# Two-layer adaLN trunk on one core: modulation vectors collected in the rows of one tile and transposed once per sublayer, attention's products regrouped, gate columns in a tile of their own

## The chip, the cores and the metric

The kernel runs on one core of a Trainium2 chip. The metric is the device time of one execution in microseconds (us), the median of several. TensorE (PE) multiplies, VectorE (DVE) and ScalarE (ACT) do elementwise work, SyncE (SP) issues the loads.

## The reference, cut to what matters

One sequence of 256 tokens, width 1024, float32, two layers. Each layer is FFN, token mixing, FFN; each sublayer normalizes, applies a shift and a scale, and adds its result under a gate. Shift, scale and gate come from a vector c (adaLN): nine vectors of 1024 a layer, each a product of silu(c) with a 1024 x 1024 matrix.

```python
mod = (jax.nn.silu(c) @ ada_w[l] + ada_b[l]).reshape(B, 3, 3, 1, D)
n = _modulate(_rmsnorm(h, norm_g[l, 0]), mod[:, 0, 0], mod[:, 0, 1])
h = h + 0.5 * mod[:, 0, 2] * _swiglu(n, ffn_w_in[l, 0], ffn_w_out[l, 0])
n = _modulate(_rmsnorm(h, norm_g[l, 1]), mod[:, 1, 0], mod[:, 1, 1])
z = n @ mix_w_in[l]
zq, zkv, zg, zuv, zga, zgb = jnp.split(z, IN_SPLITS, axis=-1)
...
nsa_gates = jax.nn.sigmoid(zg).reshape(B, S, NSA_HEADS, 3)
y_a = _nsa(q, kv[:, :, 0], ..., nsa_gates, ...)      # 8 heads, 3 branches
y_b = _gmlp(zuv, ...)                                # u * (W_s v + b)
merged = jax.nn.sigmoid(zga) * (y_a @ proj_a[l]) + jax.nn.sigmoid(zgb) * (y_b @ proj_b[l])
h = h + mod[:, 1, 2] * (merged @ w_out[l])
n = _modulate(_rmsnorm(h, norm_g[l, 2]), mod[:, 2, 0], mod[:, 2, 1])
h = h + 0.5 * mod[:, 2, 2] * _swiglu(n, ffn_w_in[l, 1], ffn_w_out[l, 1])
```

The FFN is 2816 wide (SwiGLU). zg has 24 columns, zuv 1024 (u and v).

## The kernel before, in words

**Products.** An fp32 product is made of three matmuls on split operands: weight and activation are each cut into `hi` (rounded) and `lo` (the rest), and hi·hi, hi·lo and lo·hi are summed in PSUM. Most matmuls move 256 columns (the tokens) against a 128x128 weight block.

**Stream.** The class Stream loads the weights, 128x1024 pieces of 512 KB, through 18 slots W and 8 slots X (some 1088 wide, since the v weights were 1072 columns). SP issues the loads in the order of the list of items. `_split` makes hi on ACT (L134) and lo on DVE (L135), a few weights ahead of their use. Among the weights stand *ada items*: 512 KB of an adaLN matrix, which DVE multiplies with a column of silu(c) and adds to an accumulator (L252 the first, L255 the seven others of a set). The table `ada_plan` says in which sublayer (0 to 5: FFN, mix, FFN, FFN, mix, FFN) the items of which set are streamed, and `interleave` spreads them between two positions of the list.

**Sets.** A complete set waits in `ready`. `ada_step` is called between an FFN's groups of matmuls: it has four matmuls sum the accumulator over the partitions (L282; the profile counts eight), ACT copies the sum to a tile `adas` (L286), and the next call has PE transpose that tile twice (L267) and DVE add the bias, giving the tile `md` (L271). There are 16 such sets.

**FFN.** `in_mm` (L617) makes two products of 24 matmuls into a bank R, `out_mm` (L563) adds 24 matmuls into the banks A, in turn. **Entering a sublayer** (`enter`): h is updated from the banks A, products with uhi/ulo (L456, 258 columns) start on a not yet normalized h while the statistics are made, and `top` and `bottom` (L487, L488, L491) then make nhi and nlo from h and the row `rsb` (ACT, L475).

**Mix.** `tok_mm` (L796) makes q, k, v for 128 tokens at a time; v's weights held 536 columns, as two products of 268, the last 24 of them the gate. `blk_mm` (L809) and `proj_mm` (L1011) make the other projections and fill PE between the steps of attention. Attention runs over pairs `pr` of heads: `st_scores` (L1116), softmax on DVE and ACT (L1125, L1127), `st_scale` (L1135 to L1139), `st_trans` (L1144), `st_pv` (L1154, L1156). The constants of a layer (w1, wsT, ln, bs) lie in slots X and were loaded together near the end of the FFN ahead of the mix; wsT is masked by L966.

**What sets the order.** PE, SP and GpSimd run in the order of the program text. On DVE and ACT a scheduler orders the work by readiness and priority.

```python
        for pr in range(9):
            if pr >= 1:
                for i in (2 * pr - 2, 2 * pr - 1):
                    st_trans(i)
            if pr < 8:
                st_scores(pr)
...
            next(fill)
...
            if pr >= 1:
                for i in (2 * pr - 2, 2 * pr - 1):
                    st_pv(i)
```

## Time and profile before

| what | value |
|---|---|
| median of 3 runs | 1154.71 us (1152.73 to 1157.96) |
| profiled execution | 1160.77 us, its span 1159.0 us |
| mean granted TensorE clock | 0.987 |
| first FFN / entering / mix 0 | 64 to 216 / 216 to 229 / 229 to about 400 us |
| second and third FFN | 417 to 594 and 607 to 782 us |
| mix 1 / last FFN | 782 to about 964 / 976 to 1147 us |
| read from HBM | 275.49 MB, 239 GB/s over the span |

The span is what the profiler recorded between the first and the last instruction; 1.8 us of that execution lie around it. Views of the profile name instructions by engine and line (L617), with the output and inputs of the program (`R<-nhi,hi`), and `x48` is a count. The ends of matmuls are modelled, so the pace of matmuls is read from their starts: the pieces of the chain that ended last follow each other without a gap, and a piece's time divided by its count is the step from one matmul to the next. A wait's row names who waited for whose result.

### The profile page before, as it was taken

To read this page: it belongs to the slowest core of one execution; us is meant where nothing else is said; L and a number is where in the kernel's file an instruction comes from. 1 tells how busy PE (TensorE), PEld (TensorE's weight loads), DVE (VectorE), ACT (ScalarE), POOL (GpSimd) and SP (SyncE) were. 2 spreads that over 40 slices of the span, in tenths; PEclk is the share of its full clock that TensorE was granted. 3 is DMA by queue.
4 is the path that set the end of the run, shared out by engine and by line. 5 is a ranking of instruction groups with operands and counts; after the bars stand their busy time and mean duration, and the time that the engine had idled before them with its cause. 6 is when DMAs were issued, how large, how long until landed. Compare 5 with 4: busy or idle time off the path is not lost. (4 is left out here: it accounts for less than half of the span.)

```text
span 1159.0 us, 23635 instructions
## 1 busy us (share of the span) xinstructions
PE 1137.9 (98%) x9630; PEld 1096.2 (95%) x9630; DVE 879.7 (76%) x1514; ACT 599.4 (52%) x1020; POOL 9.6 (1%) x13
## 2 busy tenths in 40 slices
PE   8999999989899999999999999999999999999998
PEld 6999999979799999999999999998899899999998
DVE  4998786778977799777579977767886778856543
ACT  3474444655575575444465444356656647544432
POOL 0000000000000000000000000000000000000000
PEclk8999999999999999999999999999999999999998
DMA  9979598438744659987647977974443366766600
GB/s 364 406 255 379 213 356 318 171 114 312 271 161 144 242 195 374 334 296 282 243 159 278 372 264 275 360 284 149 183 147 127 119 224 223 259 215 242 223 26 37
DMA packets 77180, 278.07 MB, mean 240 GB/s; under 512 B 8592, under 2 KB 9104, under 8 KB 77072
## 3 DMA queue, kind: packets, MB, share of 16 engines
q1 hardware_dynamic: 77072, 276.57, 65.1%
q8 instruction: 75, 1.23, 0.4%
q14 instruction: 33, 0.27, 0.1%
HBM read 275.49 MB, written 1.05 MB: 239 GB/s over the span
## 5 line engine op out<-in xcount | busy, mean ns | idle before, releaser
L135 DVE TENSOR_TENSOR lo<-raw,hi 128x1024 fp32r<-128x1024 f32 (+1 forms) x366 | 443.0, 1217 | 127.2 <-ACT hi L134 107.0
L134 ACT ACTIVATE hi<-raw 128x1024 fp32r<-128x1024 f32 (+1 forms) x366 | 381.0, 1052 | 273.3 <-PE R L617 67.0
L563 PE MATMUL A<-s1r,hi 128*128 128x256 f32 x1408 | 255.2, 279 | 0.0
L617 PE MATMUL R<-nhi,hi 128*128 128x256 f32 x1152 | 229.6, 281 | 0.0
L617 PE MATMUL R<-nhi,lo 128*128 128x256 f32 x1152 | 227.1, 279 | 0.0
L617 PE MATMUL R<-nlo,hi 128*128 128x256 f32 x1152 | 226.8, 279 | 0.0
L563 PEld LDWEIGHTS A<-s1r,hi 128*128 128x128 f32 x1408 | 218.9, 189 | 0.2 <-DVE s1r L555 0.2
L563 PE MATMUL A<-s1r,lo 128*128 128x256 f32 x704 | 196.0, 278 | 0.0
L617 PEld LDWEIGHTS R<-nhi,hi 128*128 128x128 f32 x1152 | 174.8, 188 | 5.8 <-issue 5.8
L617 PEld LDWEIGHTS R<-nlo,hi 128*128 128x128 f32 x1152 | 175.3, 189 | 0.0
L617 PEld LDWEIGHTS R<-nhi,lo 128*128 128x128 f32 x1152 | 175.0, 189 | 0.0
L255 DVE SCALAR_TENSOR_TENSOR acc<-raw,sc,acc 128x1024 f32<-128x1024 f32 x112 | 143.4, 1281 | 24.5 <-DMA raw<-in_ada 23.7
L563 PEld LDWEIGHTS A<-s1r,lo 128*128 128x128 f32 x704 | 132.3, 188 | 0.0
L583 ACT ACTIVATE s<-R 128x256 f32<-128x256 f32 x75 | 28.3, 377 | 105.1 <-PE R L617 105.1
L809 PE MATMUL A<-nhi,hi 128*128 128x256 f32 x256 | 74.8, 292 | 0.0
L809 PE MATMUL A<-nhi,lo 128*128 128x256 f32 x256 | 71.8, 280 | 0.0
L809 PE MATMUL A<-nlo,hi 128*128 128x256 f32 x256 | 71.8, 280 | 0.0
L554 ACT ACTIVATE s1r<-s 128x256 fp32r<-128x256 f32 x88 | 36.2, 412 | 47.9 <-DVE s L585 46.7
L585 DVE TENSOR_TENSOR s<-s,R 128x256 f32<-128x256 f32 x75 | 31.2, 416 | 37.1 <-ACT s L583 37.0
L809 PEld LDWEIGHTS A<-nhi,hi 128*128 128x128 f32 x256 | 49.0, 191 | 3.9 <-issue 2.3
L809 PEld LDWEIGHTS A<-nhi,lo 128*128 128x128 f32 x256 | 48.7, 190 | 0.0
L809 PEld LDWEIGHTS A<-nlo,hi 128*128 128x128 f32 x256 | 48.6, 190 | 0.0
(258 smaller groups left out, 1627.5 us busy)
## 6 DMA issues: line engine op xcount, KB each, us to landing
raw<-in_win SPq DMA_DIRECT2D x170, 512.0 KB, 5.7
raw<-in_ada SPq DMA_DIRECT2D x144, 512.0 KB, 5.7
raw<-in_mixw SPq DMA_DIRECT2D x92, 512.0 KB, 3.6
raw<-in_wou SPq DMA_DIRECT2D x88, 512.0 KB, 5.4
raw<-in_mixv SPq DMA_DIRECT2D x8, 536.0 KB, 5.7
w<-in_w SPq DMA_DIRECT2D x8, 512.0 KB, 8.5
raw<-in_win SPq DMA_DIRECT2D x8, 384.0 KB, 9.8
h<-in_xT SPq DMA_DIRECT2D x2, 512.0 KB, 5.5
```

The source lines that it names most:

```text
L134: self.nc.scalar.activation(hi[:, :n], raw[:, :n], AF.Copy)
L135: self.nc.vector.tensor_sub(lo[:, :n], raw[:, :n], hi[:, :n].bitcast(F32))
L255: V.scalar_tensor_tensor(a, raw[:, :D], sc[:, kb:kb + 1], a, op0=ALU.mult, op1=ALU.add)
L554: A.activation(hi_out, src, AF.Copy)
L563: T.matmul(accs[db // 2][:, (db % 2) * S:(db % 2 + 1) * S], w[:, db * 128:(db + 1) * 128], xx, start=(first and i == 0 and p == 0 and db % ...
L583: A.activation(s_, r[:, 0:S], AF.Silu)
L585: V.tensor_mul(g_, s_, r[:, S:2 * S])
L617: T.matmul(r[:, ab * S:(ab + 1) * S], W[:, c0:c0 + 128], xx[:, k], start=(i == 0 and ab == 0), stop=(i == 23), skip_group_check=True)
L809: T.matmul(r[:, b * S:(b + 1) * S], w[:, k], xx[:, k], start=(b == 0 and k == 0 and p == 0), stop=(k == 7 and p == 2), skip_group_check=True)
```

## The change

1. **Sets.** The sum of a set is now made with `hot`, a tile of zeros with one column of ones: its shifted slice puts the k-th set of the sublayer in row k of each 32-row group. The first set is copied by ACT into the tile `rows["t"]`, later ones are added to it by DVE. `ada_flush` transposes that tile once per sublayer, ahead of the FFN's last product (in a mix, within its output product), and makes all `md` tiles.
2. **Plan.** The first FFN streams five sets (it had four), mix 0 one (it had two), spread over more of its weights.
3. **Layer constants.** Only mp is loaded in the FFN; w1 goes into the mix's list at position 5, wsT, ln and bs at position 9.
4. **Gate.** v's weights are 512 columns, one product; the gate's 24 columns (padded to 32) are a weight tile of 128x256 with hi and lo in one slot. Its result is computed as 64 x 256 and brought to tokens by two small matmuls, `gzs` between them.
5. **Attention.** `st_pv` of pair pr − 2, `st_trans` of pr − 1 and `st_scores` of pr now follow each other, then both fills. `st_scale` treats both heads of a pair in one reciprocal and one product.
6. **Slots.** All slots are 1024 wide. The four X0, X1, X2, X5 take raw weights alone. `top` reads the row in PSUM and no longer waits for ACT's copy.

```diff
+EVEN_SLOTS = ("X0", "X1", "X2", "X5")
...
-            sh, hi = self._take(f"hi{i}", F32R, n)
-            sl, lo = self._take(f"lo{i}", F32R, n)
-            self.nc.scalar.activation(hi[:, :n], raw[:, :n], AF.Copy)
-            self.nc.vector.tensor_sub(lo[:, :n], raw[:, :n], hi[:, :n].bitcast(F32))
+            sh, hi = self._take(f"hi{i}", F32R)
+            sl, lo = self._take(f"lo{i}", F32R) if n > 256 else (None, hi)
...
+            self.nc.scalar.activation(hv, rv, AF.Copy)
+            self.nc.vector.tensor_sub(lv, rv, hv.bitcast(F32))
...
+    hot = cp.tile([128, 64], F32, name="hot")
+    V.memset(hot, 0.0)
+    V.memset(hot[:, 31:32], 1.0)
...
     def ada_step(now=False):
 
         clock[0] += 1
-        while summed:
-            si, m, sm = summed.pop(0)
+        while ready and (now or clock[0] >= ready[0][2]):
+            si, m, _ = ready.pop(0)
+            k = len(summed)
             p = rbank()
-            for f in range(2):
-                T.transpose(p[:, f * 128:(f + 1) * 128], sm[:, f * 128:(f + 1) * 128], ident)
+            for t in range(4):
+                T.matmul(p[32 * t:32 * t + 32, 0:256], hot[:, 31 - k:63 - k], acc[si, m][:, t * 256:(t + 1) * 256],
+                         start=True, stop=True, tile_position=(0, 32 * t))
             with tc.high_priority(PRIO_M):
+                if k == 0:
+                    rows["t"] = tp.tile([128, 256], F32, tag="adas", name=f"adas{si}_{m}")
+                    A.activation(rows["t"], p[:, 0:256], AF.Copy)
+                else:
+                    V.tensor_add(rows["t"], rows["t"], p[:, 0:256])
+            summed.append((si, m))
+
+    def ada_flush():
+
+        p = rbank()
+        for f in range(2):
+            T.transpose(p[:, f * 128:(f + 1) * 128], rows["t"][:, f * 128:(f + 1) * 128], ident)
+        with tc.high_priority(PRIO_M):
+            for k, (si, m) in enumerate(summed):
...
-        while ready and (now or clock[0] >= ready[0][2]):
-            si, m, _ = ready.pop(0)
-            p = rbank()
-            for t in range(4):
-                T.matmul(p[32 * t:32 * t + 32, 0:256], ones[:, 0:32], acc[si, m][:, t * 256:(t + 1) * 256],
-                         start=True, stop=True, tile_position=(0, 32 * t))
-            sm = tp.tile([128, 256], F32, tag="adas", name=f"adas{si}_{m}")
-            with tc.high_priority(PRIO_M):
-                A.activation(sm, p[:, 0:256], AF.Copy)
-            summed.append((si, m, sm))
...
-    ada_plan = {0: [(0, 2), (1, 0), (1, 1), (1, 2)], 1: [(2, 0), (2, 1)], 2: [(2, 2), (3, 0), (3, 1), (3, 2)],
+    ada_plan = {0: [(0, 2), (1, 0), (1, 1), (2, 0), (2, 1)], 1: [(1, 2)], 2: [(2, 2), (3, 0), (3, 1), (3, 2)],
...
-        ws = interleave(ws, extra, *((20, 18) if kind == "mix" else ((12 if idx == 0 else 14), 6)))
+        if kind == "mix":
+            ws = interleave(ws, extra, MIX_A, len(ws) - MIX_B)
+            ws.insert(9, layer_loads(idx, 2))
+            ws.insert(5, layer_loads(idx, 1))
+        else:
+            ws = interleave(ws, extra, 10 if idx == 0 else 14, 6)
         if kind == "ffn" and idx % 2 == 0:
-            ws.insert(len(ws) - 8, layer_loads(idx // 2))
+            ws.insert(len(ws) - 8, layer_loads(idx // 2, 0))
...
-            V.scalar_tensor_tensor(tt_[db], h[:, db], A_[:, db:db + 1], rsb, op0=ALU.mult, op1=ALU.mult)
+            V.scalar_tensor_tensor(tt_[db], h[:, db], A_[:, db:db + 1], aux[:, 256:512], op0=ALU.mult, op1=ALU.mult)
...
-                ada_step()
+                ada_step(k >= NF - TAIL)
+        if summed:
+            ada_flush()
         out_mm(*range(NF - GROUP, NF))
...
-            tok_mm(vb, 536, c, st.next(), [(0, 268), (268, 268)])
+            tok_mm(vb, 512, c, st.next(), [(0, 512)])
+
+        gz = bank("A1")
+        W = st.next()
+        wg = W[0][:, 0:512].rearrange("p (k c) -> p k c", c=64)
+        for k in range(8):
+            for p in range(2):
+                T.matmul(gz[0:64, 0:S], wg[:, k], x[p][:, k], start=(k == 0 and p == 0), stop=(k == 7 and p == 1),
+                         skip_group_check=True)
...
+        gzs = tp.tile([64, 256], F32, tag="s1", bufs=8, name=f"gzs{l}")
+        A.activation(gzs, gz[0:64, 0:S], AF.Copy)
...
+        for tt in range(2):
+            T.matmul(gz[:, 256 + tt * 24:280 + tt * 24], gzs[:, tt * 128:(tt + 1) * 128], cst_t[0:64, C_SEL:C_SEL + 24],
+                     start=(tt == 0), stop=True, skip_group_check=True)
...
-        for pr in range(9):
-            if pr >= 1:
+        for pr in range(10):
+            if pr >= 2:
+                for i in (2 * pr - 4, 2 * pr - 3):
+                    st_pv(i)
...
+            if 1 <= pr < 9:
                 for i in (2 * pr - 2, 2 * pr - 1):
                     st_trans(i)
             if pr < 8:
                 st_scores(pr)
-                for i in (2 * pr, 2 * pr + 1):
-                    st_scale(i)
+                st_scale(pr)
...
-        acc_mm(accs, Ws, False, True, lambda db: ada_step(db == 2) if db in (0, 2, 4) else None)
+        acc_mm(accs, Ws, False, True, lambda db: ada_step(True) if db == 0 else ada_flush() if db == 3 and summed else None)
```

What this does to the order shows at three places. The first is PE in the attention loop of mix 0, an iteration in its middle (L809 is a block fill and L837 the same line after the change; L1154 and L1156 are pv, after the change L1199 and L1201). Before, a fill stands on both sides of pv:

```order
L809 MATMUL A_300_4047<-nlo_2956,hi_3723 128x256
L1154 MATMUL A_261_3759<-s_289_3998,VK_3244 64x256
L1156 MATMUL A_261_3759<-s_289_3998,VK_3244 64x128
L1154 MATMUL A_261_3759<-s_291_4004,VK_3244 64x256
L1156 MATMUL A_261_3759<-s_291_4004,VK_3244 64x128
L809 MATMUL A_301_4085<-nhi_2955,hi_3798 128x256
```

PE after the change, at the same place (L1189 is the transposes, L1157 the scores):

```order
L837 MATMUL A_292_4034<-nlo_2974,hi_3770 128x256
L1199 MATMUL A_258_3738<-s_282_3957,VK_3292 64x256
L1201 MATMUL A_258_3738<-s_282_3957,VK_3292 64x128
L1199 MATMUL A_258_3738<-s_284_3963,VK_3292 64x256
L1201 MATMUL A_258_3738<-s_284_3963,VK_3292 64x128
L1189 MATMUL R_293_4066<-cst_t,s_288_3976 128x128 x3
L1189 MATMUL R_295_4072<-cst_t,s_289_3981 128x128 x3
L1157 MATMUL R_297_4078<-VK_3292,qT_3279 128x128
```

Pv moved from between two fills to ahead of the transposes and scores; the two fills then follow each other. The second place is DVE in the first iteration of that loop, from the scaling of the first probabilities on. Before (L252 and L255 are ada items, L135 lo splits, L1138 and L1139 the scaling):

```order
L252 TENSOR_SCALAR acc_1_3716<-raw_3598,sc 128x1024
L1138 TENSOR_SCALAR s_266_3774<-s_266_3774,rc_3785 128x128
L1135 RECIPROCAL rc_3790<-nmax_3779 128x2
L1139 TENSOR_SCALAR s_266_3774<-s_266_3774,rc_3785 128x256
L1136 TENSOR_TENSOR rc_3790<-rc_3790,gts_3424 128x2
L555 TENSOR_TENSOR ybl_3712<-s_257_3707,ybh_3711 128x512
L1138 TENSOR_SCALAR s_268_3780<-s_268_3780,rc_3790 128x128
L1139 TENSOR_SCALAR s_268_3780<-s_268_3780,rc_3790 128x256
L255 SCALAR_TENSOR_TENSOR acc_1_3716<-raw_3604,sc,acc_1_3716 128x1024
L135 TENSOR_TENSOR lo_3724<-raw_3673,hi_3723 128x1024
```

and after (L265 is an ada item, L142 a lo split, L1183 and L1184 the scaling):

```order
L265 SCALAR_TENSOR_TENSOR acc_2_3215<-raw_3593,sc,acc_2_3215 128x1024
L1178 RECIPROCAL rc_3763<-nmax_3752 128x4
L1180 TENSOR_TENSOR rc_3763<-rc_3763,gts_3416 128x4
L142 TENSOR_TENSOR lo_3810<-raw_3665,hi_3809 128x1024
L1183 TENSOR_SCALAR s_263_3753<-s_263_3753,rc_3763 128x128
L1184 TENSOR_SCALAR s_263_3753<-s_263_3753,rc_3763 128x256
L1183 TENSOR_SCALAR s_264_3758<-s_264_3758,rc_3763 128x128
L1184 TENSOR_SCALAR s_264_3758<-s_264_3758,rc_3763 128x256
L142 TENSOR_TENSOR lo_3886<-raw_3706,hi_3885 128x1024
```

The items there are one per iteration instead of two to three, and the half of gMLP's split (L555) left that place. The third place is DVE where mix 0 is entered. Before, one lo split (L135) stands there, ahead of the statistics (L400) and the modulated rows (L487, L491):

```order
L135 TENSOR_TENSOR lo_3012<-raw_2671,hi_3011 128x1024
L400 TENSOR_SCALAR var_2896<-A_182_2893 128x2
L414 TENSOR_SCALAR s_185_2924<-cst_t,rstd_2898 128x128 x2
L487 SCALAR_TENSOR_TENSOR s_187_2957<-h,md_1_2357,rsb_2929 128x256 x2
L487 SCALAR_TENSOR_TENSOR s_188_2962<-h,md_1_2357,rsb_2929 128x256 x2
```

After (L142 splits, L1007 the mask on wsT, L513 the modulated rows):

```order
L142 TENSOR_TENSOR lo_3024<-raw_2659,hi_3023 128x1024
L426 TENSOR_SCALAR var_2914<-A_180_2911 128x2
L142 TENSOR_TENSOR lo_3037<-raw_2673,hi_3036 128x1024
L440 TENSOR_SCALAR s_183_2942<-cst_t,rstd_2916 128x128 x2
L142 TENSOR_TENSOR lo_3069<-raw_2797,hi_3068 128x1024
L1007 TENSOR_TENSOR wsT_3029<-wsT_3029,cst_t 128x1024
L513 SCALAR_TENSOR_TENSOR s_185_2975<-h,md_1_2737,A_180_2911 128x256 x2
```

Three splits and the mask now stand there, and the modulated rows read PSUM (A) instead of rsb.

## What I predict

> **What bounds the kernel now.** The profile's page is read first: busy times, and the groups and transfers that carry prices below.
>
> ```profile
> PE 1137.9 (98%) x9630; PEld 1096.2 (95%) x9630; DVE 879.7 (76%) x1514; ACT 599.4 (52%) x1020; POOL 9.6 (1%) x13
> L135 DVE TENSOR_TENSOR lo<-raw,hi 128x1024 fp32r<-128x1024 f32 (+1 forms) x366 | 443.0, 1217 | 127.2 <-ACT hi L134 107.0
> L563 PE MATMUL A<-s1r,hi 128*128 128x256 f32 x1408 | 255.2, 279 | 0.0
> L617 PE MATMUL R<-nhi,hi 128*128 128x256 f32 x1152 | 229.6, 281 | 0.0
> L563 PE MATMUL A<-s1r,lo 128*128 128x256 f32 x704 | 196.0, 278 | 0.0
> L255 DVE SCALAR_TENSOR_TENSOR acc<-raw,sc,acc 128x1024 f32<-128x1024 f32 x112 | 143.4, 1281 | 24.5 <-DMA raw<-in_ada 23.7
> L585 DVE TENSOR_TENSOR s<-s,R 128x256 f32<-128x256 f32 x75 | 31.2, 416 | 37.1 <-ACT s L583 37.0
> raw<-in_mixw SPq DMA_DIRECT2D x92, 512.0 KB, 3.6
> ```
>
> TensorE (PE) is busy 98% of the span, so time can only come from how fast it steps, and from its few waits. The list of PE's waits comes second (us in total, times, longest):
>
> ```profile
> PE R L1144 <- DVE s L1138: 4.7, 2, 4.4
> PE A L796 <- DVE lo L135: 3.5, 3, 2.3
> ...
> PE R L456 <- DVE lo L135: 1.0, 1, 1.0
> ...
> PE R L456 <- ACT hi L134: 0.8, 1, 0.8
> PE A L617 <- ACT nhi L488: 0.6, 1, 0.6
> ```
>
> Then the chain that ended last, in order of time (start, us, what), around the last ada set:
>
> ```profile
> 1101.76 5.44 PE R L617 x48
> ...
> 1109.92 0.57 PE R L282 x8
> 1110.49 5.65 PE R L617 x48
> 1116.14 2.73 PE A L563 x24
> 1118.87 0.22 PE R L267 x2
> 1119.09 16.96 PE R L617 x144
> ```
>
> The same 256-column matmul has two paces. Before the transposes of L267 it steps every 5.44/48 = 113.3 ns; the set's sums (L282) leave that as it is. After the two transposes it steps every 16.96/144 = 117.8 ns, 4% slower, until something else interrupts. The table by windows, PE alone, over every stretch of the four FFNs with the slow pace (19 windows; the first, the longest, the last), and one fast stretch:
>
> ```profile
> 126.40:143.10 16.70, 16.70 (x145) 1.00 0.57 209
> ...
> 607.20:652.00 44.80, 44.80 (x383) 1.00 0.84 320
> ...
> 1119.10:1147.30 28.20, 28.20 (x242) 1.00 0.00 1
> sum 318.40, PE 318.40; mean PE 16.76
> 976.70:1109.80 133.10, 133.10 (x1176) 1.00 0.63 224
> ```
>
> Granted clock is 1.00 in both, so this is no throttling. Of these stretches 12 begin behind a pair of transposes, 6 behind a set's sums that were entered slow, and one (607.2) with the sublayer.
>
> The table by windows (span, PE busy, PEld, DVE, ACT, POOL, clock, DMA share, GB/s) for the two attention loops, three stretches at half clock, and two FFNs:
>
> ```profile
> 293.20:380.50 87.30, 82.64 (x687) 75.50 (x687) 73.31 (x200) 54.95 (x131) 0.00 (x0) 0.96 0.53 182
> 862.40:941.60 79.20, 79.20 (x685) 73.06 (x685) 56.81 (x177) 49.59 (x124) 0.00 (x0) 1.00 0.37 128
> 242.10:245.60 3.50, 3.50 (x23) 2.38 (x25) 2.34 (x3) 2.13 (x3) 0.00 (x0) 0.51 0.12 47
> 313.80:320.60 6.80, 5.65 (x28) 4.92 (x29) 6.76 (x18) 2.56 (x4) 0.00 (x0) 0.50 0.94 313
> 788.30:791.70 3.40, 3.40 (x18) 3.40 (x18) 3.40 (x9) 1.75 (x3) 0.00 (x0) 0.50 0.01 2
> 64.00:215.00 151.00, 150.99 (x1309) 148.61 (x1309) 121.60 (x145) 72.01 (x107) 0.00 (x0) 1.00 0.81 299
> 607.00:782.00 175.00, 175.00 (x1512) 172.28 (x1513) 142.08 (x175) 80.63 (x117) 0.00 (x0) 1.00 0.82 305
> ```
>
> A wait of 2.3 us (L796) or more is followed by some 3.4 us at clock 0.5, so each such wait costs about 1.7 us more than the list says.
>
> **The change, part by part.** The sum is made on the profiled execution, 1160.8 us, 6.1 us above the median of 1154.7; the same gain is then taken from the median.
>
> (A) Pace. Transposes stay only in a flush, ahead of the last 48 matmuls of a sublayer; the sums leave a fast stretch fast. All slow stretches at the fast pace: 318.4 × (1 − 113.3/117.8) = 12.2 us. Four flushes leave 48 matmuls slow each, 4 × 48 × 4.5 ns = 0.9. The stretch from 607.2 to the first transposes at 661 (some 53 us, 2.0 us of gain) began slow without transposes, behind the nhi wait of 0.6, and I leave it. **−9.3**; ends 0 and −12.2.
>
> (B) Sixteen pairs of transposes become five: 11 × 0.22 = **−2.4**. In exchange eleven sets are added to the row tile on DVE, which the nearest row (L585, 128x256 with a PSUM input) puts at 0.42 us each; they lie beside PE, which needs the tile only at the flush. Without that cover a flush would wait 0.4.
>
> (C) Attention of mix 0. Equal matmuls (x687, x685) take 87.3 us there and 79.2 in mix 1, which has no ada items. Sixteen items fall ahead of and into its first iterations; DVE fills 6.76 of 6.80 us there, and the transposes wait 4.4 us for the scaled probabilities. Eight items remain, one per iteration as the order shows. One iteration then asks DVE for about 1.28 + 2 × 1.22 beside its softmax; mix 1 pays 56.8/79.2 of the time without the item, and 7 × 1.28 = 9 us more is 83%. **−8.1**; ends 0 and −8.1.
>
> (D) Starts of the mixes. The first projections (L796) wait three times, 3.5 us in all, for a lo split that stands behind the normalization on DVE: twice at mix 0, the longer 2.3, and once at mix 1. The 2.3 is followed by 3.5 us at half clock (1.75): 5.25. The splits now stand ahead of it, three of them, as the order shows. What is late next: wsT, whose mask multiply (L1007, the old L966, formerly inside the FFN, a 128x1024 operation like L135's 1.2 us) now stands between the splits and the first modulated rows. Its load goes out when the FFN's last product frees a slot. The 96 entering matmuls, twice the 5.79 us quoted under rival 4, come before the rows, and a load lands in 3.6 us (in_mixw): several us to spare. If it came later than that, PE would wait as long. I take **−4.7**, a short wait left over (ends −5.25, +3). Entering mix 1, the fourth weight's hi and lo came amid the h updates: waits 0.8 and 1.0 and 1.7 of half clock; they now come ahead of them: **−3.5** (ends 0, −3.5).
> The Trainium skill, "TensorE: Matmul & The Clock Gate", Part 1, has the clock fall only behind an idle window of some 3.4 us. By it the half clock behind 2.3 us has another cause and may stay, and its −4.7 would be −2.95 (the sum −25.6); the trace shows half clock behind every wait of that size, and the sum goes by the trace.
>
> (E) Attention order. One iteration of mix 1 from the chain:
>
> ```profile
> 895.54 0.66 PE R L1144 x6
> ...
> 896.98 2.94 PE A L809 x24
> 899.92 0.59 PE A L1154 x4
> 900.50 0.22 PE A L1156 x4
> 900.72 3.02 PE A L809 x24
> ...
> 917.39 0.84 PE R L1144 x6
> ...
> 828.58 11.77 PE A L796 x93
> ```
>
> The 24 matmuls behind pv take 3.02 us: 24 × 117.8 = 2.83 and 0.19 of re-entry. At the fast pace they are 24 × 113.3 = 2.72. With pv, transposes and scores in a row, the second fill continues the first: −0.30 at best; if the 0.19 only moves to the joint between pv and transposes, −0.11. I take −0.2 × 16 iterations = −3.2. What it adds: transposes now wait for a softmax covered by two fills alone. With 24-matmul fills that is 5.7 us, enough; with the 12-matmul fills at the end of the loop, where the row of 0.84 against 0.66 already waits 0.18, the cover falls by pv's 0.8 us, so +0.2 to +0.5, twice per layer: +0.8 to +2. **−2.4**; ends −4.8 and +2.
> The Trainium skill, "TensorEngine Tiling (Array Packing)", Key Properties, says that a change of tiling mode, not of tile, drains TensorE. There are four changes of mode per iteration before and after (scores use 64 rows, pv 64 columns), so by it no joint is saved and (E) would be 16 × −0.11 + 0.8 = −1; the trace's re-entry of 0.19 behind pv agrees.
>
> (F) V and gate. The v product was 96 matmuls of 268 columns, 11.77/93 = 126.6 ns each, 12.1 us a layer. It becomes 48 of 512 columns. The nearest row of that width:
>
> ```profile
> 815.50:826.50 11.00, 11.00 (x48) 1.00 0.19 69
> ```
>
> so 48 take 11.0. The gate adds 16 at 113 ns (1.8), two small matmuls (0.3) and a wait for the copy between them (ends 0 and 1, taken 0.5; four key transposes lie in between, and behind the waiting pair stand PE's block fills, which need nothing of it). 11.0 + 2.6 − 12.1 = +1.5 a layer: **+3.0** (ends +2, +5).
>
> The sum: −9.3 − 2.4 − 8.1 − 4.7 − 3.5 − 2.4 + 3.0 = **−27.4**: 1133.4 for a profiled execution like this one, 1127.3 against the median, written as 1127.
>
> **The rivals.**
> 1. **The slow pace stays.** That transposes set it is a correlation: 12 of 15 followed, and 607.2 began slow with none. If a set's own sums or the sublayer's start set it, (A) is 0: 1137 us. If today's fast FFN stretches turn slow too (1408 + 704 + 3 × 1152 = 5568 matmuls in the groups quoted, three equal products of L617, less 318.4/0.1178 = 2700 slow ones: 2870 × 4.5 ns = 13): 1150.
> 2. **The first FFN becomes bound by its stream.** It takes 40 items for 32: DVE 121.6 + 8 × 1.28 = 132 of 151 us, 87%. Against it: the third FFN carries 40 at 81% with PE busy 175.00 of 175.00. For it: its window is shorter. Each stall would be like that at mix 1's start, 1.8 + 1.7 us; three are 10.5: 1138; with rival 1, 1147.
> 3. **The moves trade wait for wait:** wsT late, transposes late by 0.5 us in all 16 iterations (+8), the mixes' starts not cured ((D) 0, so +8.2), (C) half (+4): 1127.3 + 20.2 = 1147.5.
> 4. **Slower: a third pace.** All slots become 1024 wide, so weights and moving tiles lie at other addresses. This row of 258-column matmuls shows that such a pace exists:
>
> ```profile
> 964.19 5.79 PE R L456 x48
> ```
>
> 5.79/48 = 120.6 ns, 2.4% over the slow pace for 0.8% more columns. If the layout set it for the 5568 FFN matmuls, each would lose 5.1 ns against the mean of the two paces (115.5): +28, with (A) lost: 1127.3 + 9.3 + 28.4 = 1165. It decides the sign from some 3500 matmuls on (18.1/5.1 ns). Against it: sums and products of one layout already run at both paces, so the pace is not the layout's alone.
> 5. **It doesn't do what it says:** the scheduler's DVE order could undo the placement; the order shows the splits and items moved, so only their arrival is open: within 0.5%, 1152.
>
> **How the numbers follow.** Forecast 0.50 (its own range 1117 to 1135), rival 1 0.22, rival 2 0.08, rival 3 0.08, rival 4 0.06, rival 5 0.06. A measurement of this kernel can tell about 0.5% from no change, 5.8 us: faster is below 1149, slower above 1160.5. Faster: 0.50, most of rival 1 (0.18) and of 2 (0.07), a third of 3 (0.03) = 0.78. Slower: rival 4 and a rest of 3, 0.08. Same: 0.14. The best ends of all terms (−12.2 − 2.4 − 8.1 − 5.25 − 3.5 − 4.8 + 2 = −34.3) give 1120, a little more room below for paces I can't see: 1116. Above, the range takes in rivals 1 and 2 together: 1148.
>
> **What would show it.** (A): in the chain, FFN stretches of 5.44 us per 48 right up to the flush; 5.65 there would refute it. (B): L267's line with a third of its count. (C): mix 0's loop within 2 us of mix 1's, no wait of the transposes for the scaling over 1 us. (D): no L796 or L456 entry above 0.5 in the list of waits and no clock of 0.5 at the mixes' starts; an L1007 wait for wsT's DMA would be the failure. (E): an iteration of 7.9 to 8.1 us. (F): v and gate near 13.6 us a layer. The prediction is wrong if the paces follow something else than the transposes, since a third of the gain hangs on them.

## The result, and the profile after

The changed kernel takes 1126.44 us (median of 4 runs, 1125.87 to 1127.76) beside 1156.34 us for the kernel before (1152.73 to 1158.89): a ratio of 0.9745, 95% interval 0.9714 to 0.9776. A second set of runs gave 1126.84 us and 0.9738 (0.9706 to 0.977). The forecast was 1127 us. The time is right, and so are most of the sums; two of the reasons given for them are not, as the experiments show.

The whole list of PE's waits after the change (us in total, times, longest):

```profile
PE R L715 <- DVE s L713: 2.0, 1, 2.0
PE A L773 <- ACT nhi L762: 1.5, 1, 1.5
PE R L434 <- DVE ones L234: 1.1, 1, 1.1
PE R L733 <- DVE md L759: 0.9, 1, 0.9
PE A L441 <- DVE s L440: 0.8, 1, 0.8
PE R L746 <- ACT s L740: 0.5, 1, 0.5
PE A L643 <- ACT nhi L514: 0.4, 1, 0.4
PE A L896 <- issue: 0.3, 1, 0.3
```

The waits for splits (formerly L796, L456) and for the scaled probabilities (L1144) are gone; five of the eight rows lie ahead of the first FFN. The chain that ended last, around the last set (L278 the sums, L292 the flush; L643 and L589 are the old L617 and L563):

```profile
1075.70 0.57 PE R L278 x8
1076.27 5.65 PE R L643 x48
1081.92 2.72 PE A L589 x24
1084.64 16.32 PE R L643 x144
1100.96 5.45 PE A L589 x48
1106.41 0.22 PE R L292 x2
1106.63 5.48 PE A L589 x48
```

16.32 us for 144 matmuls are 113.3 ns each, where the same stretch took 16.96. Behind the flush the pace is fast here too (5.48 for 48). Of the five flushes only that of the second FFN left its last 48 matmuls slow (117.8 ns by their starts).

The table by windows after the change (us, PE, PEld, DVE, ACT, POOL, clock, DMA share, GB/s): the two attention loops, the first product of mix 0, the entering of mix 1, and the four FFNs:

```profile
285.70:363.00 77.30, 77.30 (x683) 71.33 (x683) 58.65 (x167) 49.60 (x124) 0.00 (x0) 1.00 0.47 164
829.70:907.00 77.30, 77.30 (x684) 71.37 (x684) 53.88 (x161) 50.12 (x124) 0.00 (x0) 1.00 0.41 137
224.10:235.20 11.10, 11.10 (x50) 8.87 (x48) 8.57 (x24) 11.00 (x18) 0.00 (x0) 1.00 0.45 171
756.40:768.90 12.50, 12.50 (x107) 12.50 (x107) 11.73 (x26) 10.33 (x18) 1.54 (x1) 1.00 0.69 207
65.80:211.70 145.90, 145.89 (x1292) 143.00 (x1291) 126.88 (x158) 68.60 (x104) 0.00 (x0) 1.00 0.92 338
398.30:571.20 172.90, 172.48 (x1524) 170.14 (x1524) 138.29 (x181) 85.52 (x125) 0.00 (x0) 1.00 0.81 293
583.60:756.40 172.80, 172.80 (x1532) 170.11 (x1531) 143.94 (x186) 82.04 (x119) 0.00 (x0) 1.00 0.82 307
942.30:1124.30 182.00, 177.71 (x1547) 176.76 (x1546) 106.81 (x148) 78.51 (x115) 0.69 (x1) 0.97 0.49 168
```

The same stages of the kernel before, in that order from the first product of mix 0 on:

```profile
229.00:244.80 15.80, 12.86 (x50) 9.36 (x48) 11.29 (x27) 13.41 (x21) 0.00 (x0) 0.92 0.42 162
784.95:801.20 16.25, 14.45 (x106) 14.04 (x105) 10.43 (x26) 8.39 (x17) 0.69 (x1) 0.89 0.12 43
67.80:216.50 148.70, 148.69 (x1290) 146.31 (x1289) 119.34 (x146) 70.12 (x106) 0.00 (x0) 1.00 0.80 294
417.10:593.70 176.60, 176.60 (x1530) 174.43 (x1529) 136.06 (x175) 85.63 (x125) 0.00 (x0) 1.00 0.78 282
606.90:784.90 178.00, 178.00 (x1538) 175.28 (x1539) 144.89 (x183) 83.58 (x125) 0.00 (x0) 1.00 0.83 306
976.50:1159.00 182.50, 178.39 (x1548) 177.45 (x1546) 108.10 (x149) 79.19 (x115) 0.69 (x1) 0.98 0.48 170
```

So the FFNs gave 2.8, 3.7, 5.2 and 0.5 us (12.2 in all), mix 0's loop 10.0 (87.3 to 77.3), mix 1's 1.9, the first product of mix 0 4.7, the entering of mix 1 3.8. Between these two profiled executions the span fell by 34.7 us, between the medians by 29.9: the profiled execution of the kernel before (1160.8) was a long one among the 1149.7 to 1162.3 us that its runs here have shown, while the changed kernel stays within 2.2 us.

### The profile page after: what moved, and what is told of

Its sections match the earlier page's. It is cut to its first block, busy times and chain, and to the rows that moved or that the text cites. A ratio compares the mean times of both kernels' runs of the same rounds, so it can differ in the third digit from the quotient of the medians.

```text
span 1124.3 us, 23469 instructions
## 1 busy us (share of the span) xinstructions
PE 1112.5 (99%) x9552; PEld 1070.5 (95%) x9552; DVE 874.7 (78%) x1497; ACT 597.3 (53%) x1007; POOL 10.8 (1%) x13
## 5 line engine op out<-in xcount | busy, mean ns | idle before, releaser
L142 DVE TENSOR_TENSOR lo<-raw,hi 128x1024 fp32r<-128x1024 f32 x366 | 443.1, 1215 | 118.4 <-ACT hi L141 76.5
L141 ACT ACTIVATE hi<-raw 128x1024 fp32r<-128x1024 f32 x368 | 381.5, 1048 | 234.0 <-PE R L643 57.9
L589 PE MATMUL A<-s1r,hi 128*128 128x256 f32 x1408 | 251.6, 277 | 0.0
L643 PE MATMUL R<-nhi,hi 128*128 128x256 f32 x1152 | 226.0, 277 | 0.0
L643 PE MATMUL R<-nlo,hi 128*128 128x256 f32 x1152 | 224.2, 276 | 0.0
L643 PE MATMUL R<-nhi,lo 128*128 128x256 f32 x1152 | 224.2, 276 | 0.0
L589 PEld LDWEIGHTS A<-s1r,hi 128*128 128x128 f32 x1408 | 217.2, 188 | 0.6 <-ACT hi L141 0.4
L589 PE MATMUL A<-s1r,lo 128*128 128x256 f32 x704 | 194.5, 276 | 0.0
L643 PEld LDWEIGHTS R<-nhi,hi 128*128 128x128 f32 x1152 | 173.5, 188 | 5.8 <-issue 5.8
L643 PEld LDWEIGHTS R<-nlo,hi 128*128 128x128 f32 x1152 | 173.4, 188 | 0.0
L643 PEld LDWEIGHTS R<-nhi,lo 128*128 128x128 f32 x1152 | 173.3, 188 | 0.0
L265 DVE SCALAR_TENSOR_TENSOR acc<-raw,sc,acc 128x1024 f32<-128x1024 f32 x112 | 143.3, 1279 | 7.9 <-DMA raw<-in_ada 7.5
L589 PEld LDWEIGHTS A<-s1r,lo 128*128 128x128 f32 x704 | 132.2, 188 | 0.0
L837 PE MATMUL A<-nhi,hi 128*128 128x256 f32 x256 | 72.7, 284 | 0.0
L837 PE MATMUL A<-nlo,hi 128*128 128x256 f32 x256 | 70.8, 277 | 0.0
L837 PE MATMUL A<-nhi,lo 128*128 128x256 f32 x256 | 70.8, 277 | 0.0
L837 PEld LDWEIGHTS A<-nhi,hi 128*128 128x128 f32 x256 | 48.1, 188 | 2.1 <-issue 0.3
L837 PEld LDWEIGHTS A<-nhi,lo 128*128 128x128 f32 x256 | 48.2, 188 | 0.0
L837 PEld LDWEIGHTS A<-nlo,hi 128*128 128x128 f32 x256 | 48.1, 188 | 0.0
```

The source lines that it names most:

```text
L141: self.nc.scalar.activation(hv, rv, AF.Copy)
L142: self.nc.vector.tensor_sub(lv, rv, hv.bitcast(F32))
L265: V.scalar_tensor_tensor(a, raw[:, :D], sc[:, kb:kb + 1], a, op0=ALU.mult, op1=ALU.add)
L589: T.matmul(accs[db // 2][:, (db % 2) * S:(db % 2 + 1) * S], w[:, db * 128:(db + 1) * 128], xx, start=(first and i == 0 and p == 0 and db % ...
L643: T.matmul(r[:, ab * S:(ab + 1) * S], W[:, c0:c0 + 128], xx[:, k], start=(i == 0 and ab == 0), stop=(i == 23), skip_group_check=True)
L837: T.matmul(r[:, b * S:(b + 1) * S], w[:, k], xx[:, k], start=(b == 0 and k == 0 and p == 0), stop=(k == 7 and p == 2), skip_group_check=True)
```

## The experiments

Two ideas were open: what sets the pace of 256-column matmuls, and which edit cured the waits at the starts of the mixes. Times are medians; the changed kernel's 1126.84 us is the mark (the first run below), and each has its ratio to the kernel before on its own chip. The kernel before had medians of 1155.72 to 1157.45 us on these chips, and the mark was run on the first of them only, so a difference of 2 us or less is not certain.

One thing varies between the profiled runs with no plain link to the edit: the pace at which an FFN begins. The first FFN begins fast in the mark and slow in the runs with the old plan, with moved slots (both), with the old slot rule and with the copied row; the second begins slow in those with the old attention order, with the old loads, with slots moved by 64 bytes, with the old slot rule and with the copied row. Such a beginning, 360 to 456 matmuls at 4.5 ns more, is worth 1.6 to 2.1 us.

**The changed kernel again.** No edit.

> The changed kernel once more, as the mark beside which the others of this chip are read: 1126 to 1128 us if the result holds, 0.9745 of the kernel before within its interval.

1126.84 us, 0.9738 (0.9706 to 0.977). The mark stands.

**Each set turned in the next step, in the changed kernel.**

```diff
-            for t in range(4):
-                T.matmul(p[32 * t:32 * t + 32, 0:256], hot[:, 31 - k:63 - k], ...)
+        while summed:
+            si, m, sm = summed.pop(0)
+            p = rbank()
+            for f in range(2):
+                T.transpose(p[:, f * 128:(f + 1) * 128], sm[:, f * 128:(f + 1) * 128], ident)
...
-        if summed:
-            ada_flush()
```

> The changed kernel, but each set is transposed in the step behind its sum, as before, ahead of the next in-product. Theory (transposes ahead of an in-product set the slow pace of 117.8 ns, which then stays): terms A and B of the prediction come back, +9.3 and +2.4, about 1138 us, and the FFN stretches behind a pair step at 117.8. Rival (the new slot layout made the pace fast): only B comes back, 1129 us, stretches at 113.3.

1131.43 us, 0.9779 (0.9744 to 0.9814): 4.6 more, between what the two theories gave. Windows of 8 us behind four successive pairs of the first FFN, PE alone, all of one length so that the count tells the pace:

```profile
118.00:126.00 8.00, 8.00 (x70) 1.00 0.86 306
135.90:143.90 8.00, 8.00 (x73) 1.00 0.61 206
161.20:169.20 8.00, 8.00 (x70) 1.00 0.83 311
179.10:187.10 8.00, 8.00 (x73) 1.00 0.98 343
```

Slow, fast, slow, fast (8000/70 is 114 with the edges, 8000/73 is 110). By the starts in the trace, all sixteen pairs found the fast pace, and they left slow and fast strictly in turn; the sums that found the slow pace (six) left the fast one each time. So transposes do set the slow pace here, but only every other time. Neither theory holds as stated: the pace is a state that an interruption may change, and as all pairs found the same pace, something besides the pace ahead decides what they leave.

**The sets turned once, in the kernel before.**

```diff
-    xp_.tile([128, 48], F32, tag="pad", name="pad")
+    hot = xp_.tile([128, 48], F32, tag="pad", name="pad")
...
+        if summed:
+            ada_flush()
         out_mm(*range(NF - GROUP, NF))
```

(with the new `ada_step` and `ada_flush`; the one in `hot` stands in column 4, so that it fits where padding was).

> The kernel before, with nothing changed but that the sets go into rows of one tile and are transposed once per sublayer; slots, plan, loads, gate and attention stay. Theory (transposes set the pace): A and B alone, 11.7 us off, about 1144.5 us against 1156.3. Rival (layout): 1154 us, the FFN stretches still slow.

1148.99 us, 0.9927 (0.9899 to 0.9954), over ten runs from 1141.68 to 1154.11: 8.3 off the 1157.31 of its chip, and a wide spread. Its profiled execution, the longest, shows where time is left (windows of PE alone: the start of the first FFN and of the second):

```profile
68.20:118.00 49.80, 49.80 (x425) 1.00 0.88 320
417.00:468.00 51.00, 51.00 (x453) 1.00 0.84 317
```

117 ns and 113 ns; the third FFN, entered behind its nhi wait, begins at 117 too. With few interruptions left, an FFN mostly keeps the pace it begins with: the first and the third stay slow through the sums of three sets, and the fourth's turn them fast. In the kernel before, the first FFN's profiled start was fast; here it is slow. The flush alone takes away what makes the pace slow, but not what lets it begin slow.

**Weight slots moved by 64 bytes.**

```diff
-        pool.tile([128, 16], F32, tag="pad", name="pad_w")
+        pool.tile([128, 32], F32, tag="pad", name="pad_w")
```

> The changed kernel with 64 bytes more ahead of the weight slots, so that weights lie elsewhere relative to the moving tiles; the order is the same, instruction by instruction. Theory (addresses do not set the pace): 1126.8 us. Rival (layout sets it, rival 4 of the prediction): another pace in the FFN stretches, 117.8 or 120.6 instead of 113.3 ns, up to 1126.8 + 5568 x 7.3 ns = 1167 us.

1138.49 us, 0.9826 (0.9796 to 0.9855): 11.7 more with the same instructions in the same order on PE, DVE and ACT; only addresses differ. The pad stands in the pool of the weights, behind the slots X0, X1, X2 and X5. Whether the pools made after that one, with the moving tiles, moved along isn't on record, so which distance matters stays open. Windows of PE alone, on both sides of the sums of a set in the third FFN:

```profile
665.00:688.00 23.00, 23.00 (x206) 1.00 0.64 237
690.00:713.00 23.00, 23.00 (x197) 1.00 0.85 305
```

Here the *sums* leave the slow pace (206 matmuls in 23 us ahead, 197 behind), which they never did in the profile of the changed kernel (sixteen of sixteen left the fast one). In the FFNs no third pace appears, but the last fills of the attention loops step at 118.7 ns on average by their starts (907 to 916 us), more than the slow pace. The first FFN took 149.6 us, the second 176.8 and the third 175.5, where the changed kernel has 145.9, 172.9 and 172.8: 10.3 us more, some 3.7 of it from the slow beginnings of the first two, which other runs show without the move. Each attention loop takes 0.9 more.

**The same, moved by 128 bytes.**

```diff
-        pool.tile([128, 16], F32, tag="pad", name="pad_w")
+        pool.tile([128, 48], F32, tag="pad", name="pad_w")
```

> The changed kernel with 128 bytes more ahead of the weight slots (the run before had 64 and took 1138.5 us, with 2460 slow matmuls in its long stretches). Theory a (only the position within 128 bytes relative to the moving tiles decides how an interruption leaves the pace): back to 1126.8 us and fast stretches. Theory b (any move of the slots draws the states anew): slow stretches in some FFNs, 1130 to 1140 us.

1128.66 us (1125.94 to 1130.9), 0.9767 (0.9725 to 0.9808). Its fastest run equals the mark; in the profiled one, its longest, the stretches behind both attention loops were slow and so was the first FFN's start. Nearer to theory a: most of the loss of 64 bytes is gone at 128. But the position within 128 bytes is not all: both attention loops took 77.98 us by their starts, and every loop of a run with the new order and the slots unmoved took 77.27, but for mix 0 under the old plan.

**The turning step ahead of the out-product.**

```diff
             for k in outs_after(si, j):
+                ada_step(k >= NF - TAIL)
                 out_mm(k)
                 if k < NF - TAIL:
                     st.more()
-                ada_step(k >= NF - TAIL)
```

> As the run that turns each set in the step behind its sum (1131.4 us, 8 of its 15 pairs followed by the slow pace), but the step stands ahead of the out-product instead of behind it. Theory a (which product follows the transposes decides the pace): stretches stay at 113.3 and only the transposes' own time comes back, about 1129 us. Theory b (the pace is a state that passes from one interruption to the next, whatever product follows): about half of the stretches slow again, 1131 us, slow and fast in a regular turn.

1133.39 us (1131.42 to 1135.03), 0.979 (0.9766 to 0.9814). Theory a falls: the place does not save the pace. Behind the first pairs of the second FFN, again in windows of 8 us:

```profile
463.50:471.50 8.00, 8.00 (x70) 1.00 0.79 279
498.20:506.20 8.00, 8.00 (x73) 1.00 0.96 331
```

Slow and fast, as in the run that turns each set. Theory b's regular turn does not hold throughout: in the first FFN the first three pairs all left the slow pace, and the sums of the fourth set found it slow and left it so (117.7 ns by the starts).

**Three kinds of interruption.**

```diff
+            kind = "..... pspstststpsps"[j] if si in (2, 5) and j < 18 else "."
+            if kind == "s":
+                for g in range(2):
+                    T.matmul(rbank()[:, 0:S], x[0][g * 64:g * 64 + 64, 0, 0:128], x[0][g * 64:g * 64 + 64, 1], ...)
+            elif kind == "p":
+                    T.matmul(p[g * 64:g * 64 + 64, 0:S], h[:, 0, 0:64], h[:, 1], ..., tile_position=(0, g * 64))
+            elif kind == "t":
+                    T.transpose(p[:, f * 128:(f + 1) * 128], h[:, 0, f * 128:(f + 1) * 128], ident)
```

> The changed kernel with thirteen small interruptions in each of the second and the last FFN, one behind the groups j = 5 to 17, of three kinds: s, two matmuls on half the rows like those of the scores; p, two matmuls onto half the columns like pv; t, two transposes as of a set. Nothing reads their results. Theory a (the kind of an interruption decides, as the attention loops suggest): every s leaves 113.3 ns, every p 117.8, t about half of each. Theory b (the state ahead of it and the interruption decide together, as the runs that turn each set suggest): one kind leaves both paces, in a pattern that follows the pace ahead of it. In time about 26 x 0.4 us and the slow stretches, some 1140 us.

1139.51 us, one run. The string in the edit holds a blank at j = 5, so there are twelve interruptions in each of the two FFNs, behind j = 6 to 17. The last FFN, PE alone, windows of 8 us behind s, t, s, t, t and p (the s between the two last t's left a fast one too):

```profile
1002.00:1010.00 8.00, 8.00 (x73) 1.00 0.70 226
1027.90:1035.90 8.00, 8.00 (x70) 1.00 0.52 189
1036.90:1044.90 8.00, 8.00 (x70) 1.00 0.70 234
1045.70:1053.70 8.00, 8.00 (x73) 1.00 0.52 182
1062.70:1070.70 8.00, 8.00 (x70) 1.00 0.80 256
1072.20:1080.20 8.00, 8.00 (x72) 1.00 0.63 197
```

From the second window on, t turned the pace from fast to slow, s left it slow, t turned it fast, the next s left it fast, t turned it slow and p turned it fast. In the second FFN the two s that found the slow pace differ from each other:

```profile
488.20:496.20 8.00, 8.00 (x72) 1.00 0.75 271
505.60:513.60 8.00, 8.00 (x70) 1.00 0.74 267
```

By the starts the 72 matmuls behind them took 8.29 us, fast, and 8.68, slow. Theory a falls, and of theory b only half holds: one kind leaves both paces, but the kind and the pace ahead do not decide alone. Only t turned a fast stretch slow in this run; p, behind which nearly every fill of the attention loops was slow in the kernel before (the prediction's row of 3.02 us for 24), left none slow here. What else decides isn't shown; the runs with moved slots say that addresses have a part in it.

**The old order in the attention loop.**

```diff
-        for pr in range(10):
-            if pr >= 2:
-                for i in (2 * pr - 4, 2 * pr - 3):
-                    st_pv(i)
+        for pr in range(9):
...
+            if pr >= 1:
+                for i in (2 * pr - 2, 2 * pr - 1):
+                    st_pv(i)
```

> The changed kernel with the old order in the attention loop (transposes and scores, fill, pv, fill). By the prediction's term E 2.4 us more, 1129 us; if a change of tiling mode costs the same wherever it stands, and only the pace differs, 1 us more; by the starts of the attention loops in the two traces (79.1 and 77.3 us in mix 1) 1.8 us per layer and 0.85 of pace behind the loop, about 5 us more, 1131 us.

1133.97 us, 0.9802 (0.9767 to 0.9837): 7.1 more. By the starts of its stages the loops take 2.4 and 2.1 us more, the products behind them 0.6 and 0.85 more, both from pace, and the second FFN 2.7 more, since it began slow (172.9 in the mark, 175.6 here); the start and the last stages took some 2 less. The order pays in the products right behind its loop, as the pace that it leaves goes on. Whether the slow second FFN belongs to it isn't shown: that FFN also began slow in the run with the old loads, where the loop and the products behind it were as fast as in the mark.

**The old plan of ada items.**

```diff
-    ada_plan = {0: [(0, 2), (1, 0), (1, 1), (2, 0), (2, 1)], 1: [(1, 2)], ...
+    ada_plan = {0: [(0, 2), (1, 0), (1, 1), (1, 2)], 1: [(2, 0), (2, 1)], ...
...
-            ws = interleave(ws, extra, MIX_A, len(ws) - MIX_B)
+            ws = interleave(ws, extra, 20, 18)
```

> The changed kernel with the old plan of ada items: the first FFN streams four sets, mix 0 two, spread between the old positions. Theory (term C: two to three items per attention iteration fill DVE and make the transposes wait): mix 0's attention loop goes from 77.3 back to about 85 us with a wait of some 4 us and half clock, in all +8, 1135 us. Rival (the regrouped order and the paired scaling of attention already cover the burst): the loop stays within 1 us of mix 1's, 1127 us.

1131.19 us (1128.65 to 1134.5), 0.9773 (0.9746 to 0.9801): 4.4 more. The list of waits, and the loop of mix 0 with a stretch inside it, of its longest run:

```profile
PE R L1189 <- DVE s L1183: 4.6, 1, 4.6
```

```profile
288.90:372.80 83.90, 79.31 (x684) 73.08 (x684) 66.49 (x175) 53.63 (x128) 0.00 (x0) 0.96 0.53 186
309.00:313.00 4.00, 3.05 (x17) 2.51 (x18) 3.99 (x8) 2.77 (x4) 0.00 (x0) 0.50 1.01 389
```

83.9 against 77.3: the wait of the transposes for the scaling and the half clock behind it are back, with DVE full (3.99 of 4.00). The theory holds in the profiled run, which is the longest of four; its first FFN, which began slow, took 2.05 more than in the mark as well. The median says that it cost less in others, of which there is no trace.

**All constants loaded in the FFN again.**

```diff
-            ws.insert(9, layer_loads(idx, 2))
-            ws.insert(5, layer_loads(idx, 1))
...
-            ws.insert(len(ws) - 8, layer_loads(idx // 2, 0))
+            n8 = len(ws) - 8
+            for part in (2, 0, 1):
+                ws.insert(n8, layer_loads(idx // 2, part))
```

> The changed kernel with all constants of a layer loaded together near the end of the FFN ahead of the mix, as before. Theory (term D: the six slots that they take there, and the later weights, are what left the splits behind the normalization): waits of the first projections at mix 0 (3.1 us and 1.75 of half clock) and of the entering products at mix 1 (1.8 and 1.7) return, +5 to +8.3, 1132 to 1135 us. Rival (the plan of items or the row read from PSUM cured the starts, not the loads): at most +1, 1127 to 1128 us.

1136.12 us, 0.9808 (0.9785 to 0.9832): 9.3 more, but not where expected. Its list of waits has none at the starts of the mixes (the first product of mix 0 belongs to a stage of 61.1 us, 61.3 in the mark), and a new one, at 191 us in the first FFN:

```profile
PE R L643 <- ACT hi L141: 5.8, 1, 5.8
```

```profile
185.00:200.00 15.00, 8.74 (x67) 8.25 (x67) 6.81 (x7) 3.97 (x5) 0.00 (x0) 0.86 1.03 371
```

DMA is busy the whole time there (1.03 of the time, 371 GB/s; the mark has 0.97 and 376 in the same window, and PE waits for nothing): with five sets the first FFN has no room for the constants as well, as it had with four in the kernel before. It takes 155.1 us by the starts, 9.2 more than in the mark: the wait, the half clock behind it and a second wait of 0.5. So the spread of the loads pays for the fifth set; it did not cure the starts.

**The old rule for taking slots.**

```diff
-        return len(self._fit(False)) >= (2 if len(self._fit(True)) > len(self._fit(False)) else 3)
+        return n <= SLOTS[s] and (s not in self.extras or self.lend)
...
-        ws += [("w", mixv[l, k], 1024) for k in range(4)]
+        ws += [("w", mixv[l, k], 1024, 1) for k in range(4)]
```

(an item with the mark counts as 1072 wide and needs three free slots of the wide half, as before; the tiles themselves stay 1024. The run undoes the rest of the rule too: every load needs three free slots, where two can do in the changed kernel, and X0, X1, X2 and X5 take hi and lo again.)

> The changed kernel with the old rule for taking slots: the four v weights count as 1072 wide and fit only into half of the slots, though all tiles stay 1024. Theory (the rule held back weights, so that the third split at a mix's start came behind the normalization on DVE): the first projections of mix 0 wait about 3.1 us and run 3.5 us at half clock again, 15.8 us where they take 11.1, and entering mix 1 16.2 instead of 12.4: +4.7 + 3.8, 1135 us. Rival (another part of the change cured the starts): within 1 us of 1126.8.

1170.93 us, 1.0138 (1.0102 to 1.0173): 44 us more, slower than the kernel before. Waits, and the windows of entering mix 0 and of its products up to attention:

```profile
PE R L488 <- ACT hi L147: 7.5, 2, 5.4
PE A L830 <- DVE lo L148: 6.2, 4, 2.7
```

```profile
216.20:237.70 21.50, 15.67 (x106) 15.17 (x105) 12.86 (x28) 9.28 (x18) 0.70 (x1) 0.76 0.47 160
237.80:304.50 66.70, 63.00 (x445) 54.56 (x443) 52.59 (x104) 39.25 (x61) 0.69 (x1) 0.97 0.57 199
```

The waits of the first products (four, 6.2 us) are those of the kernel before, and stronger, and so are those on entering mix 1. The wait on entering mix 0 (5.4) is new: the kernel before took 12.4 us there, without one. By the starts of the stages the mixes' beginnings account for 23 us (9.1 and 5.5 in mix 0, 5.2 and 3.5 in mix 1), and the FFNs for 20 more, three of them at the slow pace for long stretches (178.7, 178.7 and 187.3 us where the mark has 172.9, 172.8 and 181.6). The old rule with the new loads is worse than either kernel, so 44 us is not the rule's price in the kernel before; but the rule makes these waits. Which part of it does (the width, the count of free slots, or the use of the four X slots) was not tried apart. The pace, too, behaves differently with other slots: seven times it stepped at 120 ns for some 24 matmuls (at 989.6 us, for one), and in the last FFN it went from 113 over 120 to 118 ns with nothing between the products.

**The row from ACT's copy again.**

```diff
-            V.scalar_tensor_tensor(tt_[db], h[:, db], A_[:, db:db + 1], aux[:, 256:512], op0=ALU.mult, op1=ALU.mult)
+            V.scalar_tensor_tensor(tt_[db], h[:, db], A_[:, db:db + 1], rsb, op0=ALU.mult, op1=ALU.mult)
```

> The changed kernel with the modulated rows made from ACT's copy of the row, as before, and not from PSUM. The order on DVE stays. Theory (the copy lies on the way to nhi only where PE runs out of entering products): 0.3 to 0.8 us more at each of the four entries behind a first FFN, 1128 to 1130 us, and where an FFN is entered behind a gap it may start at the slow pace, 2 us more. Rival (covered): 1126.8 us.

1129.21 us (1128.24 to 1132.79), 0.9785 (0.9748 to 0.9822): 2.4 more. Its list of waits has none at the entries that the mark lacks, and all four take 12.4 to 13.0 us as there; what its profile has more are two FFNs that begin slow, 504 matmuls in the first and 456 in the second (2.4 and 1.5 us by the starts of the stages). No copy was found to cost anything by itself, and 2.4 us is near what a change of chip can do.

## Why the prediction was right, and where not

**(A), pace, −9.3 forecast.** The four FFNs gave 12.2. Counted by starts, 2688 of their matmuls were slow before and 48 are now: 2640 × 4.5 ns = 11.9 of pace. (B) is within the 12.2 as well (10 of 11 pairs, 2.2); a fifth set in the first FFN, a wait of 0.4 in the second and the last FFN's end, among others, take 1.9 back. The pace gave more than forecast, since the third FFN too began fast, for which I had set nothing, and four of five flushes cost no pace. The size was right to within the stated ends. The reason, that transposes set the slow pace and their absence keeps it fast, is half of it. With each set turned again the changed kernel loses 4.6, not 11.7; the kernel before with the flush gains 8.3, with a spread of 12 us; and 64 bytes of address alone bring 11.7 back without one transpose more. Shown: pace is a state that outlasts the interruption; interruptions change it, the same kind now one way and now the other; addresses have a part in which way; with fewer interruptions and this layout it stays fast in the changed kernel. Not shown: what the state is, what decides it, and how much of the 11.9 belongs to the flush and how much to the layout. That the layout came out well is luck: nothing in the forecast rested on it.

**Rival 4** named the layout as a possible cause and was given 0.06. Its price was too high: for 256 columns a third pace showed only in places, 118.7 ns in the last fills of the run moved by 64 bytes and 120 ns in seven stretches of the run with the old slot rule. Its cause is real, and this layout happens to stand on the good side.

**(B), −2.4.** The chain has one pair of 0.22 us at the flush it shows; the sums there cost the same 0.57. As worked out.

**(C), −8.1.** Mix 0's loop fell by 10.0, mix 1's, where no items were, by 1.9; the difference is 8.1. The old plan brings back the wait (4.6) and the half clock, 6.6 of the 8.1 in the profiled run. Confirmed by its mechanism.

**(D), −4.7 and −3.5.** Measured 4.7 at mix 0's first product (15.8 to 11.1), 1.2 at mix 1's (12.26 to 11.10 by the starts of the stages), 3.8 on entering mix 1 (16.25 to 12.5). The sizes were right, but for the 1.2, which the sum had left out; the half clock is gone with the waits (1.00 in both rows after). That the splits now stand ahead was read from the order; what put them there I had left to the text's other edits, the loads among them. The old loads leave the starts whole, and so do the old plan, the sets turned each and the copied row; of what was undone alone, only the old rule for slots brings the waits back. The likely reason is that weights 1072 wide found room in half of the slots only and held back what stood behind them; but that run undid the other parts of the rule with it, so this part is not shown alone. wsT, the feared next cause, shows in no list of waits.
One step of (D) was too simple: that half clock follows every wait of 2.3 us. The prediction's own row at 788.3 had it behind waits of 0.8 and 1.0. In the run with the old slot rule PE's starts lie 2.75 us apart at 247 us (idle for 2.35 of them) and 3.09 us apart at 815 us (idle for 2.69), and these stretches begin just behind (PE alone, clock behind the count):

```profile
250.50:254.00 3.50, 3.50 (x18) 0.63 0.00 1
818.00:821.50 3.50, 3.50 (x54) 1.00 0.00 0
```

The shorter gap cost clock and the longer did not. The Trainium skill, "TensorE: Matmul & The Clock Gate", Part 1, calls the window in which activity is judged free-running, so that the moment counts and not the length alone; the two rows agree with that. The first does not agree with its idle window of some 3.4 us as the least that costs clock, since that gap was shorter.

**(E), −2.4.** Measured 1.9 in mix 1's loop, and −3.8 if mix 0's gave the same, which cannot be told from (C) there. The part that failed is the +0.8 for transposes that wait behind the short fills: the list has no such wait. A full iteration fell from 8.21 to 8.03 us by its starts, 0.18, between the ends of 0.11 and 0.30; the rest of the 1.9 (0.6) is the loop's last fill (132 matmuls before, 120 now), slow before and fast now. What I did not count is the pace that the loop leaves behind: the products behind the loops gained 1.8 and 0.85 us (24.62 to 22.81 and 22.61 to 21.76; in the first of them also a pair of transposes and its wait), and the run with the old order gives back 0.6 and 0.85 of it.

**(F), +3.0.** From the start of V to the step behind the gate (12.48 us before, 14.17 after, in mix 0) it is:

```profile
259.32:271.80 12.48, 12.48 (x103) 1.00 1.00 386
```

```profile
249.94:264.11 14.17, 14.14 (x76) 1.00 0.82 287
```

+1.7, and +1.1 in mix 1 by the starts of the same stages (13.05 and 14.17). The term is confirmed.

**The sum.** Terms outside it came to about −4: 2.0 earlier out of the start, the two stretches behind attention, 0.75 at the third FFN's entry (the nhi wait), and +1.1 at the last entry (0.8 of it in the list, L441). They are why, with (A), (E) and the 1.2 of (D), the profiled spans fell by 34.7 and not 27.4. That the median is met within 0.6 us is then partly luck: the profiled execution of the kernel before stood 4 us above its own median, and no run here shows how much of that the slow pace made.

**Rivals 2 and 3** did not come: DVE fills 126.9 of 145.9 us of the first FFN (87%, as forecast) and PE waits nowhere in it. The run with the old loads shows how near it was: eight more loads there (3.25 MB) cost a wait of 5.8 us and 9.2 in all.

## What to carry to other kernels

Where one engine is busy 98% of the time, read its pace from starts, stretch by stretch: a few per cent can hide in a state that no list of waits shows, and a pad of 64 bytes can flip it. A planner's rule on buffers (which item fits which slot) belongs among the suspects for a wait on a split, beside the engine that the wait names. Undoing one edit at a time measures interactions, not prices: here the parts undone cost 4.6, 4.4, 7.1, 9.3, 2.4 and 44 us, in part at places that the edit doesn't name, and in part in FFNs that begin slow in one run and fast in the next.

## What the runs showed of the hardware that was not expected

- Steady matmuls of 256 columns with a new weight each run, nearly everywhere, at one of two steps, 113.3 or 117.8 ns, at granted clock 1.00, and keep it for long while nothing interrupts them (1176 matmuls in the last FFN). The exceptions: 118.7 ns in the last fills of the run moved by 64 bytes, 120 ns for seven stretches of some 24 in the run with the old slot rule, where the step also changed with no interruption.
- Two transposes, eight small sums, or two half-row matmuls can change the step or leave it. Sixteen pairs of transposes that all found the fast step left slow and fast in turn (70, 73, 70, 73 matmuls in 8 us behind the first four); two half-row pairs of one FFN that found the slow step left it fast once and slow once.
- A pad of 64 bytes more among the weight slots changed which interruption does so, and cost 11.7 us. One of 128 bytes cost 1.8; in its profiled run each attention loop took 0.7 more.
- An idle stretch of 2.35 us was followed by clock 0.63 over 3.5 us, and one of 2.69 us, in the same execution, by 1.00.
- Execution times of the kernel before spread by 6 to 10 us within a set (1149.7 to 1159.2, for one), with its sets turned once by 12 (1141.7 to 1154.1), those of the changed one by 2.2 over both its sets. That the two steps make this spread isn't shown: the run with the old slot rule has both and spreads by 2.3.
